# Forgetting attention without the row's constant in its bias, and low key halves over zeros

## The chip, the cores and the metric

The kernel runs on one core of one Trainium2 chip. The metric is the device time in microseconds (us) of one execution; the median of several runs counts. The profile shows one execution: TensorE (PE, with its weight loads as PEld), VectorE (DVE), ScalarE (ACT), GpSimd (POOL) and the queues that issue DMAs (SP among them).

## What is computed

A decoder layer on 512 tokens of width 2048: a mixer of three head groups (12 dilated attention heads "a", 8 forgetting attention heads "b", 4 heads of gated linear attention "c"), a cross-attention, and a gated MLP. All of it is in float32. The part that the change touches is forgetting attention, with heads of 64 and query blocks of 128:

```python
c = jnp.cumsum(jax.nn.log_sigmoid(f_logit.astype(jnp.float32)), axis=1)
...
logits = jnp.einsum('bihd,bjhd->bhij', qn, k,
                    preferred_element_type=jnp.float32) * HEAD_DIM ** -0.5
logits = logits + (cn[..., :, None] - cT[..., None, :])
qpos = n * BLOCK_Q + jnp.arange(BLOCK_Q)
logits = jnp.where(kpos[None, :] <= qpos[:, None], logits, -jnp.inf)
p = jax.nn.softmax(logits, axis=-1)
```

The term cn of the query's own row is the same for all keys of a row, so the softmax does not depend on it.

## The kernel before

Matrix products are made of three matmuls on operands that are split into a rounded high part and a low part (mm3, L375 to L377): high by high, low by high, high by low. Weights stream in by SP's queue; ScalarE rounds them to `whi` (L361 in the mixer, L336 in the MLP), VectorE subtracts to get `wlo` (L362, L337). Five pairs of such splits are held at a time.

The mixer projects first; attention runs behind it in the background. Each head of group a or b is a generator, attend() (L518). Two generators take turns (PAR), and the projections of the following heads call tick() every four blocks of 128 rows, which lets each of the two heads take a step. `behind()` ties each background matmul to the projection matmul ahead of it in the program, and a scheduler then sets the order on each engine; an engine takes its instructions strictly in that order. So a background matmul that has to wait holds up the projections behind it.

A head's steps. The first makes the score operands: `qs` holds the query's high half in the head's 64 rows and its low half in the other 64; `kh` holds the key's high half in both (L526, L527); `kl` holds the key's low half in both: VectorE subtracts it into the head's rows (L529), ScalarE copies it to the other rows (L530). Two matmuls of 128 rows give the scores of a block (L544, L545): the first is q high and q low by k high, the second q high and q low by k low. Then scores(t) for the query blocks t = 0 to 3 and turn(t) in the order s0, s1, t0, s2, t1, s3, t2, t3, one step each. scores(t) adds the bias and takes the row's maximum in one VectorE operation (L547), exponentiates on ScalarE (L548), and scales by the row's sum on VectorE (L549, L550). turn(t) transposes its t + 1 blocks on TensorE (L557), and ScalarE and VectorE split the result into `pth` and `ptl` (L565, L566). At the end eight matmuls multiply with the values into psO (L576, L577), which ScalarE and VectorE add into the mix (L579, L580).

The bias. Group a reads a skewed table. Group b (bias_b, L590) loads the head's cumulated gates as one row to all 128 partitions (`cb`) and builds, for each block, a tile `bb` of cb minus the constant `ci` of each query row: one operation for the blocks to the left (L599), one with the triangle `tri` for the block on the diagonal (L600). `bb` shares its four buffers with the probabilities `pt`. The constants `cnat` come from forget() (L686), a background generator of the gate stage: after the cumulated sum it gives up five turns, then transposes the sums on TensorE (L708) and copies them out on VectorE (L711). gates() (L640; four z matmuls L678, each followed by a log-sigmoid, L506 to L513, and a scan, L683) and rel_bias() (L714; matmuls L738, VectorE L739) share the turns with it.

Of the kernel before, what the change touches and what calls it, by code (L numbers as in the profile page):

```python
# [12 lines left out]
F32 = mybir.dt.float32  # L13
F32R = mybir.dt.float32r
I32 = mybir.dt.int32
AF = mybir.ActivationFunctionType
ALU = mybir.AluOpType
AX = mybir.AxisListType

P = 128  # L20
D = 2048
KT = D // P
S = 512
NT = S // P
# [3 lines left out]
DH = 64  # L28
A_HEADS = 12
B_HEADS = 8  # L30
# [37 lines left out]
PTB = 4  # L68
# [24 lines left out]
SB = 2  # L93
# [136 lines left out]
def _view(t, off, dims):  # L230
    return bass.AP(t.tensor, t.offset + off, [list(t.ap[0])] + [list(d) for d in dims])


class _Trunk:
# [283 lines left out]
    def attend(self, qf, kf, e, vv, bias_of, head, mix):  # L518
        nc, ab = self.nc, self.ab
        a = slice(DH * e, DH * e + DH)  # L520
        o = slice(DH - DH * e, 2 * DH - DH * e)
        qs = ab.tile([P, S], F32R, name="qs", tag="qs", bufs=SB)
        kh = ab.tile([P, S], F32R, name="kh", tag="kh", bufs=SB)
        kl = ab.tile([P, S], F32R, name="kl", tag="kl", bufs=SB)
        nc.scalar.activation(qs[a], qf[a], AF.Copy)
        nc.scalar.activation(kh[a], kf[a], AF.Copy)  # L526
        nc.scalar.activation(kh[o], kf[a], AF.Copy)  # L527
        nc.vector.tensor_tensor(qs[o], qf[a], qs[a].bitcast(F32), op=ALU.subtract)
        nc.vector.tensor_tensor(kl[a], kf[a], kh[a].bitcast(F32), op=ALU.subtract)  # L529
        nc.scalar.activation(kl[o], kl[a].bitcast(F32), AF.Copy)  # L530
        yield
        pth = ab.tile([P, 1280], F32R, name="pth", tag="pth", bufs=PB)
        ptl = ab.tile([P, 1280], F32R, name="ptl", tag="ptl", bufs=PB)
        nm = ab.tile([P, NT], F32, name="nm", tag="nm", bufs=3)
        sm = ab.tile([P, NT], F32, name="sm", tag="sm", bufs=3)
        pts = {}
        bias = bias_of(head)

        def scores(t):
            n = P * (t + 1)  # L540
            sc = self.pst("S")
            tt = slice(t * P, n)
            with self.behind():
                nc.tensor.matmul(sc[:, :n], qs[:, tt], kh[:, :n], start=True, stop=False)  # L544
                nc.tensor.matmul(sc[:, :n], qs[:, tt], kl[:, :n], start=False, stop=True)  # L545
            pt = pts[t] = ab.tile([P, n], F32, name="pt", tag="pt", bufs=PTB, padded_shape=[P, S])
            nc.vector.tensor_tensor_reduce(pt, sc[:, :n], bias(t), -1.0, 1e38, ALU.add, ALU.min, nm[:, t:t + 1])  # L547
            nc.scalar.activation(pt, pt, AF.Exp, scale=-1.0, bias=nm[:, t:t + 1], accum_out=sm[:, t:t + 1])  # L548
            nc.vector.reciprocal(sm[:, t:t + 1], sm[:, t:t + 1])  # L549
            nc.vector.tensor_scalar(pt, pt, sm[:, t:t + 1], None, op0=ALU.mult)  # L550

        def turn(t):
            n, pt = P * (t + 1), pts[t]
            tp = self.pst("T")
            with self.behind():
                for b in range(t + 1):
                    nc.tensor.transpose(tp[:, b * P:(b + 1) * P], pt[:, b * P:(b + 1) * P], self.ident)  # L557
            for b, step in ((0, 384), (2, 128)):
                m = min(t + 1 - b, 2)
                if m > 0:  # L560
                    at = COL[b] + (t - b) * P
                    hv = _view(pth, at, [[step, m], [1, P]])
                    lv = _view(ptl, at, [[step, m], [1, P]])
                    tv = tp[:, b * P:(b + m) * P].rearrange("p (b c) -> p b c", c=P)
                    nc.scalar.activation(hv, tv, AF.Copy)  # L565
                    nc.vector.tensor_tensor(lv, tv, hv.bitcast(F32), op=ALU.subtract)  # L566

        for f, t in ((scores, 0), (scores, 1), (turn, 0), (scores, 2), (turn, 1), (scores, 3), (turn, 2), (turn, 3)):
            f(t)
            yield  # L570
        po = self.pst("O")
        for b in range(NT):
            n = S - b * P
            st = vv[:, b, P * e:P * (e + 1)]
            with self.behind():
                nc.tensor.matmul(po[:, b * P:], st, pth[:, COL[b]:COL[b] + n], start=(b == 0), stop=False)  # L576
                nc.tensor.matmul(po[:, b * P:], st, ptl[:, COL[b]:COL[b] + n], start=False, stop=(b == NT - 1))  # L577
        tmp = ab.tile([P, S], F32, name="ot", tag="pt", bufs=PTB)
        nc.scalar.activation(tmp[a], po[o], AF.Copy)  # L579
        nc.vector.tensor_tensor(mix[a], po[a], tmp[a], op=ALU.add)  # L580
        yield
# [8 lines left out]
    def bias_b(self, h):  # L590
        nc = self.nc
        cb = self.ab.tile([P, S], F32, name="ba", tag="ba", bufs=2)
        nc.scalar.dma_start(out=cb, in_=bass.AP(self.cdr.tensor, self.cdr.offset + h * S, [[0, P], [1, S]]))

        def get(t):
            b = self.ab.tile([P, P * (t + 1)], F32, name="bb", tag="pt", bufs=PTB, padded_shape=[P, S])
            ci = self.cnat[:, t, h:h + 1]
            if t:
                nc.vector.tensor_scalar(b[:, :P * t], cb[:, :P * t], ci, None, op0=ALU.subtract)  # L599
            nc.vector.scalar_tensor_tensor(b[:, P * t:], cb[:, P * t:P * (t + 1)], ci, self.tri,  # L600
                                           op0=ALU.subtract, op1=ALU.add)
            return b

        return get

# [80 lines left out]
    def forget(self):  # L686
        nc, gl = self.nc, self.pre
        fb = self.con.tile([B_HEADS, 1], F32, name="fb")
        with self.tc.issue_after(self.begun.ins):
            nc.gpsimd.dma_start(out=fb, in_=self.d["f_bias"])  # L690
        tp = self.pst("T")
        for t in range(NT):
            nc.tensor.transpose(tp[:B_HEADS, t * P:(t + 1) * P], self.fg[:, t, :B_HEADS], self.ident)
        z = gl.tile([B_HEADS, S], F32, name="fz", tag="zs", bufs=1)
        nc.vector.tensor_scalar(z, tp[:B_HEADS, :], fb, None, op0=ALU.add)
        n = self.neg_log_sigmoid(z, [B_HEADS, S])
        one = gl.tile([B_HEADS, S], F32, name="fone", tag="zs", bufs=1)
        nc.gpsimd.memset(one, 1.0)
        cn = gl.tile([B_HEADS, S], F32, name="cn")
        nc.vector.tensor_tensor_scan(cn, one, n, 0.0, ALU.mult, ALU.add)  # L700
        self.cdr = self.dr.tile([B_HEADS, S], F32, name="cdr")
        nc.scalar.dma_start(out=self.cdr, in_=cn)
        for _ in range(5):
            yield
        tq = self.pst("T")
        with self.behind():
            for t in range(NT):
                nc.tensor.transpose(tq[:, t * B_HEADS:(t + 1) * B_HEADS], cn[:, t * P:(t + 1) * P],  # L708
                                    self.ident[:B_HEADS, :B_HEADS])
        self.cnat = self.con.tile([P, NT, B_HEADS], F32, name="cnat")  # L710
        nc.vector.tensor_copy(self.cnat, tq[:, :NT * B_HEADS].rearrange("p (t h) -> p t h", h=B_HEADS))  # L711
        yield

    def rel_bias(self):  # L714
# [178 lines left out]
    def mixer(self):  # L893
        nc, d, tc = self.nc, self.d, self.tc
# [90 lines left out]
        es_gl.close()  # L985
        self.mab = self.pool(self.es, "mab", "left")
        self.ab = self.pool(es_ab, "ab", "right")
        self.up_pre = {}
        for f in range(2, EARLY):
            self.up_sums(f)  # L990
# [870 lines left out]
```

## Time and profile before

| | us |
|---|---|
| median of 3 runs (2253.62 to 2257.49) | 2253.88 |
| the profiled execution, whole | 2255.07 |
| its span, first to last instruction | 2253.3 |
| TensorE busy in the span | 2233.6 |
| VectorE busy | 1824.1 |
| ScalarE busy | 1243.1 |
| GpSimd busy | 220.8 |

The gate stage lies at about 50 to 95 us of the span, gated linear attention up to about 320, the heads of group a from about 340 to 555, those of group b from there to 700, then the output projection, cross-attention, and the MLP from about 1000 us to the end. A matmul's busy time overlaps with the next one's, so a TensorE that is 99% busy says where it stood idle, not that every matmul ran at its best pace. The granted TensorE clock is full in all slices of the page.

### The profile page before, as it was taken

To read this page: it belongs to the slowest core of one execution; us is meant where nothing else is said; L and a number is where in the kernel's file an instruction comes from. 1 tells how busy PE (TensorE), PEld (TensorE's weight loads), DVE (VectorE), ACT (ScalarE), POOL (GpSimd) and SP (SyncE) were. 2 spreads that over 40 slices of the span, in tenths; PEclk is the share of its full clock that TensorE was granted. 3 is DMA by queue.
4 is the path that set the end of the run, shared out by engine and by line. 5 is a ranking of instruction groups with operands and counts; after the bars stand their busy time and mean duration, and the time that the engine had idled before them with its cause. 6 is when DMAs were issued, how large, how long until landed. Compare 5 with 4: busy or idle time off the path is not lost.

```text
span 2253.3 us, 42653 instructions
## 1 busy us (share of the span) xinstructions
PE 2233.6 (99%) x15902; PEld 2090.3 (93%) x15902; DVE 1824.1 (81%) x3610; ACT 1243.1 (55%) x2552; POOL 220.8 (10%) x308
## 2 busy tenths in 40 slices
PE   9999999999999999999999999999999999999997
PEld 9898898888778888889999999999999999999997
DVE  7826756666797356699999999999999998999887
ACT  7324445655575245585555555555555575747563
POOL 2000101000002011121111111111000020101003
PEclk9999999999999999999999999999999999999999
DMA  6432157322223349589777777877534493836532
GB/s 223 158 98 83 50 149 192 97 89 99 81 88 129 133 151 251 124 207 273 197 212 209 209 211 214 225 221 218 180 132 143 143 337 106 306 127 234 186 129 82
DMA packets 141843, 377.10 MB, mean 167 GB/s; under 512 B 14484, under 2 KB 53732, under 8 KB 140932
## 3 DMA queue, kind: packets, MB, share of 16 engines
q1 hardware_dynamic: 90144, 274.18, 35.0%
q0 software_dynamic: 45728, 89.86, 18.2%
q10 hardware_dynamic: 5764, 10.35, 1.4%
q8 instruction: 124, 2.03, 0.4%
q14 instruction: 83, 0.68, 0.1%
HBM read 347.28 MB, written 91.80 MB: 195 GB/s over the span
## 4 chain that ended last, share of the span: by engine, by line
PE 95%; DVE 2%; ACT 1%; issue 1%; DMA 1%; POOL 0%; DVEq 0%; POOLq 0%; ACTq 0%
PE acc L375 19%; PE acc L377 19%; PE acc L376 19%; PE psC L375 5%; PE psC L376 5%; PE psC L377 5%; PE acc L416 3%; PE acc L418 3%; PE acc L417 3%; PE psD L376 3%; PE psD L375 3%; PE psD L377 3%; PE psT L557 1%; PE psQ L375 1%; PE psS L807 1%; PE psQ L377 1%
## 5 line engine op out<-in xcount | busy, mean ns | idle before, releaser
L336 ACT ACTIVATE whi<-wraw 128x512 fp32r<-128x512 f32 (+2 forms) x814 | 466.3, 603 | 406.6 <-PE acc L376 149.4
L337 DVE TENSOR_TENSOR wlo<-wraw,whi 128x512 fp32r<-128x512 f32 (+2 forms) x814 | 517.0, 656 | 66.8 <-ACT whi L336 62.1
L375 PE MATMUL acc<-sum,whi 128*128 128x256 f32 x1956 | 541.8, 277 | 0.4 <-ACT s L1461 0.3
L377 PE MATMUL acc<-sum,wlo 128*128 128x256 f32 x1956 | 541.6, 277 | 0.3 <-DVE wlo L337 0.2
L376 PE MATMUL acc<-sum,whi 128*128 128x256 f32 x1956 | 541.3, 277 | 0.0
L362 DVE TENSOR_TENSOR wlo<-wraw,whi 128x512 fp32r<-128x512 f32 (+2 forms) x336 | 221.0, 664 | 188.6 <-ACT whi L361 187.6
L377 PEld LDWEIGHTS acc<-sum,wlo 128*128 128x128 f32 x1956 | 367.3, 188 | 1.2 <-DVE wlo L337 1.1
L375 PEld LDWEIGHTS acc<-sum,whi 128*128 128x128 f32 x1956 | 367.1, 188 | 1.2 <-ACT s L1461 0.7
L376 PEld LDWEIGHTS acc<-sum,whi 128*128 128x128 f32 x1956 | 367.3, 188 | 0.0
L361 ACT ACTIVATE whi<-wraw 128x512 fp32r<-128x512 f32 (+2 forms) x336 | 203.0, 609 | 290.7 <-PE acc L376 176.1
L375 PE MATMUL acc<-xhi,whi 128*128 128x512 f32 (+1 forms) x848 | 335.1, 395 | 0.5 <-ACT fg L938 0.5
L377 PE MATMUL acc<-xhi,wlo 128*128 128x512 f32 (+1 forms) x848 | 328.3, 387 | 0.0
L376 PE MATMUL acc<-xlo,whi 128*128 128x512 f32 (+1 forms) x848 | 328.3, 387 | 0.0
L375 PE MATMUL psC<-sum,whi 128*128 128x256 f32 x928 | 256.8, 277 | 0.0
L376 PE MATMUL psC<-sum,whi 128*128 128x256 f32 x928 | 256.7, 277 | 0.0
L377 PE MATMUL psC<-sum,wlo 128*128 128x256 f32 x928 | 256.4, 276 | 0.0
L377 PEld LDWEIGHTS acc<-xhi,wlo 128*128 128x128 f32 x848 | 159.3, 188 | 32.3
L375 PEld LDWEIGHTS acc<-xhi,whi 128*128 128x128 f32 x848 | 159.4, 188 | 29.5 <-ACT fg L938 0.9
L376 PEld LDWEIGHTS acc<-xlo,whi 128*128 128x128 f32 x848 | 159.7, 188 | 28.4 <-DVE xlo L324 0.2
L376 PEld LDWEIGHTS psC<-sum,whi 128*128 128x128 f32 x928 | 174.2, 188 | 0.0
L377 PEld LDWEIGHTS psC<-sum,wlo 128*128 128x128 f32 x928 | 174.2, 188 | 0.0
L375 PEld LDWEIGHTS psC<-sum,whi 128*128 128x128 f32 x928 | 174.2, 188 | 0.0
(406 smaller groups left out, 4340.9 us busy)
## 6 DMA issues: line engine op xcount, KB each, us to landing
wraw<-in_w_up SPq DMA_DIRECT2D x125, 512.0 KB, 6.5
b<-in_w_up SPq DMA_DIRECT2D x42, 512.0 KB, 4.9
wraw<-in_w_o SPq DMA_DIRECT2D x32, 512.0 KB, 3.5
wraw<-in_w_d SPq DMA_DIRECT2D x32, 448.0 KB, 4.4
wraw<-in_w_d SPq DMA_DIRECT2D x36, 384.0 KB, 5.4
wraw<-in_w_qka SPq DMA_DIRECT2D x24, 512.0 KB, 3.6
up<-in_w_up POOLq DMA_DIRECT2D x24, 512.0 KB, 7.3
one<-in_w_d POOLq DMA_DIRECT2D x24, 448.0 KB, 7.3
```

Of the source, the lines that this page charges most:

```text
L336: nc.scalar.activation(hi, r, AF.Copy)
L337: nc.vector.tensor_tensor(lo, r, hi.bitcast(F32), op=ALU.subtract)
L361: nc.scalar.activation(hi, r, AF.Copy)
L362: nc.vector.tensor_tensor(lo, r, hi.bitcast(F32), op=ALU.subtract)
L375: nc.tensor.matmul(out, lh, rh, start=start, stop=False, skip_group_check=more)
L376: nc.tensor.matmul(out, lh, rl, start=False, stop=False, skip_group_check=more)
L377: last = nc.tensor.matmul(out, ll, rh, start=False, stop=stop, skip_group_check=more)
L416: self.nc.tensor.matmul(o, xh[:, tt], wh, start=(k == 0), stop=False)
L417: self.nc.tensor.matmul(o, xh[:, tt], wl, start=False, stop=False)
L418: self.last = self.nc.tensor.matmul(o, xl[:, tt], wh, start=False, stop=(k == KT - 1))
L557: nc.tensor.transpose(tp[:, b * P:(b + 1) * P], pt[:, b * P:(b + 1) * P], self.ident)
L807: nc.tensor.matmul(sc[:rows, c * 64:(c + 1) * 64], kk[:, c * P:c * P + rows], qe[:, c * 64:(c + 1) * 64], start=True, stop=True)
```

## The change

Three things. The bias of group b is cb alone, without the row's constant: get(t) adds the triangle in place to the diagonal block of cb and returns a view of cb. Since that spoils the block for later rows, the query blocks of group b run from last to first (group a keeps its order). So `bb`, `cnat`, its transposes and the five turns in forget() go. And for all heads `kl` holds the low key half over 64 rows of zeros: two tiles (one for the even and one for the odd head of a pair), whose zeros VectorE writes once ahead of group a, take the place of a pool of two, and ScalarE's copy goes. Query low by key low is no longer summed in.

```diff
-        kl = ab.tile([P, S], F32R, name="kl", tag="kl", bufs=SB)
+        kl = self.kl[e]
...
         nc.vector.tensor_tensor(kl[a], kf[a], kh[a].bitcast(F32), op=ALU.subtract)
-        nc.scalar.activation(kl[o], kl[a].bitcast(F32), AF.Copy)
...
         for f, t in ((scores, 0), (scores, 1), (turn, 0), (scores, 2), (turn, 1), (scores, 3), (turn, 2), (turn, 3)):
-            f(t)
+            f(t if bias_of == self.bias_a else NT - 1 - t)
...
-            b = self.ab.tile([P, P * (t + 1)], F32, name="bb", tag="pt", bufs=PTB, padded_shape=[P, S])
-            ci = self.cnat[:, t, h:h + 1]
-            if t:
-                nc.vector.tensor_scalar(b[:, :P * t], cb[:, :P * t], ci, None, op0=ALU.subtract)
-            nc.vector.scalar_tensor_tensor(b[:, P * t:], cb[:, P * t:P * (t + 1)], ci, self.tri,
-                                           op0=ALU.subtract, op1=ALU.add)
-            return b
+            b = cb[:, P * t:P * (t + 1)]
+            nc.vector.tensor_tensor(b, b, self.tri, op=ALU.add)
+            return cb[:, :P * (t + 1)]
...
-        for _ in range(5):
-            yield
-        tq = self.pst("T")
-        with self.behind():
-            for t in range(NT):
-                nc.tensor.transpose(tq[:, t * B_HEADS:(t + 1) * B_HEADS], cn[:, t * P:(t + 1) * P],
-                                    self.ident[:B_HEADS, :B_HEADS])
-        self.cnat = self.con.tile([P, NT, B_HEADS], F32, name="cnat")
-        nc.vector.tensor_copy(self.cnat, tq[:, :NT * B_HEADS].rearrange("p (t h) -> p t h", h=B_HEADS))
...
+        self.kl = [self.ab.tile([P, S], F32R, name="kl%d" % e) for e in range(2)]
+        for kl, o in zip(self.kl, (slice(DH, P), slice(0, DH))):
+            nc.vector.memset(kl[o].bitcast(F32), 0.0)
```

The line numbers of the changed kernel are lower by 1 from L530 on, by 5 behind bias_b (L680 is L675) and by 14 behind forget() (L952 is L938). Three places show how the orders move.

The gate stage on VectorE, around the second head's scan (`gb`, L683 or L678; `ls` and `zs` are steps of the gates' log-sigmoid, `gq` is the q projection of the linear attention, evacuated from TensorE's accumulator). Before:

```order
L513 TENSOR_TENSOR ls_796<-ls_796,ls_797 96x512
L506 TENSOR_SCALAR ls_833<-zs 96x512
L683 SCALAR_TENSOR_TENSOR gb_115<-smask,ls_796 96x512
L507 SCALAR_TENSOR_TENSOR ls_834<-ls_833,zs 96x512
L362 TENSOR_TENSOR wlo<-wraw,whi 128x512
L680 TENSOR_SCALAR zs<-psO,gb 96x512
L509 TENSOR_SCALAR ls_835<-ls_834 96x512
```

In the changed kernel:

```order
L506 TENSOR_SCALAR ls_816<-zs 96x512
L507 SCALAR_TENSOR_TENSOR ls_817<-ls_816,zs 96x512
L675 TENSOR_SCALAR zs<-psO,gb 96x512
L938 SCALAR_TENSOR_TENSOR gq_116<-acc,R 96x512
L938 SCALAR_TENSOR_TENSOR gq_119<-acc,R 32x512
L513 TENSOR_TENSOR ls_778<-ls_778,ls_779 96x512
L678 SCALAR_TENSOR_TENSOR gb_115<-smask,ls_778 96x512
L362 TENSOR_TENSOR wlo<-wraw,whi 128x512
```

The evacuation of the third q projection (`gq_116`), which before stood 14 rows behind that scan, now stands ahead of the second head's L513, its scan and a split of weights; on TensorE the projection matmul that reads this `wlo` is the 15th behind the last one of the third q projection. The z matmuls also moved: the first one stands 8 projection matmuls behind the spreading of the row norm instead of 12.

The change from the first to the second pair of group b on ScalarE: the last turns of the first pair (`pth`), the operands of the second (`kh`, `kl`), the first pair's output (`ot`). Before:

```order
L526 ACTIVATE kh<-kf 64x512
L579 ACTIVATE ot<-psO 64x512
L565 ACTIVATE pth<-psT 128x2x128
L527 ACTIVATE kh<-kf 64x512
L530 ACTIVATE kl<-kl 64x512
L526 ACTIVATE kh<-kf 64x512
L565 ACTIVATE pth<-psT 128x128
L527 ACTIVATE kh<-kf 64x512
L361 ACTIVATE whi<-wraw 128x512
L565 ACTIVATE pth<-psT 128x2x128
L530 ACTIVATE kl<-kl 64x512
L565 ACTIVATE pth<-psT 128x256
```

In the changed kernel:

```order
L526 ACTIVATE kh<-kf 64x512
L527 ACTIVATE kh<-kf 64x512
L578 ACTIVATE ot<-psO 64x512
L564 ACTIVATE pth<-psT 128x2x128
L526 ACTIVATE kh<-kf 64x512
L527 ACTIVATE kh<-kf 64x512
L361 ACTIVATE whi<-wraw 128x512
L564 ACTIVATE pth<-psT 128x128
```

Both kl copies are gone, and the last turn, now that of block 0, needs one copy of 128x128 behind the split of weights, where that of block 3 needed two.

The same place on TensorE: the last turn (`psT`), and the first output matmul (`psO`) that reads its result. Before:

```order
L557 MATMUL psT<-ident,pt 128x128 x4
L375 MATMUL acc<-xhi,whi 128x512
L376 MATMUL acc<-xlo,whi 128x512
L377 MATMUL acc<-xhi,wlo 128x512
L576 MATMUL psO<-pth,vv 128x512
```

In the changed kernel:

```order
L556 MATMUL psT<-ident,pt 128x128
L375 MATMUL acc<-xhi,whi 128x512
L376 MATMUL acc<-xlo,whi 128x512
L377 MATMUL acc<-xhi,wlo 128x512
L575 MATMUL psO<-pth,vv 128x512
```

One transpose stands there instead of four; the three projection matmuls between it and the output are the same.

## The prediction

> **What bounds the kernel now.** I read the page first: the span, the busy time of the engines, and the chain of work that ended last.
>
> ```profile
> span 2253.3 us, 42653 instructions
> PE 2233.6 (99%) x15902; PEld 2090.3 (93%) x15902; DVE 1824.1 (81%) x3610; ACT 1243.1 (55%) x2552; POOL 220.8 (10%) x308
> ...
> PE 95%; DVE 2%; ACT 1%; issue 1%; DMA 1%; POOL 0%; DVEq 0%; POOLq 0%; ACTq 0%
> ```
>
> TensorE (PE) holds 95% of the chain and is idle for 19.7 us of 2253.3. The change takes work from VectorE (DVE) and ScalarE (ACT), and from TensorE four tiny transposes. So it can gain only where TensorE stands waiting for those two. Next the windows, to see how much of the idle time lies in the stages that the change touches (the columns are the stretch in us, its length, then each engine's busy time with its instructions):
>
> ```profile
> 50.00:90.00 40.00, 40.00 (x181) 32.31 (x180) 36.78 (x61) 14.86 (x25) 1.51 (x3) 1.00 0.27 94
> 320.00:340.00 20.00, 20.00 (x92) 16.73 (x91) 9.95 (x21) 8.62 (x19) 3.50 (x5) 1.00 0.77 221
> 340.00:505.00 165.00, 164.61 (x808) 137.84 (x806) 106.83 (x290) 96.67 (x226) 7.16 (x9) 1.00 0.45 125
> 505.00:555.00 50.00, 50.00 (x246) 41.78 (x245) 33.05 (x92) 29.80 (x75) 0.00 (x0) 1.00 0.28 95
> 555.00:700.00 145.00, 142.09 (x694) 115.45 (x693) 117.78 (x329) 94.59 (x219) 2.87 (x4) 1.00 0.25 86
> 730.00:740.00 10.00, 10.00 (x46) 8.29 (x45) 6.36 (x12) 3.56 (x7) 0.00 (x0) 1.00 0.57 210
> ```
>
> 50 to 90 us is the gate stage, 340 to 555 the dilated heads (group a), 555 to 700 the forgetting heads (group b), 730 to 740 a stretch of plain projections. TensorE is idle 0.39 us in the 215 us of group a and 2.91 us in the 145 us of group b. Both run the same attend(); only group b builds a bias, and there VectorE is busy 81% instead of 65%. Who is waited for in group b:
>
> ```profile
> PEld psO L576 <- ACT pth L565: 3.7, 6, 1.9
> ...
> PE psO L576 <- ACT pth L565: 1.8, 2, 1.5
> ...
> PE psT L557 <- DVE pt L550: 0.9, 3, 0.4
> ...
> PEld psS L545 <- ACT kl L530: 0.4, 1, 0.4
> ```
>
> The columns are the total, the times and the longest. Most is the output matmul psO, waiting for the ScalarE copy of the turned probabilities; one such wait is 1.5 us.
>
> Busy time hides short delays, because matmuls overlap, so 2.91 us is the lower end of what group b can give back. For the upper end I take weight loads: they fill 8.29 of 10 us in the plain stretch, where TensorE never waits, and 137.84 of 165, or 83.5%, in group a. At group a's rate 145 us would hold 121.1 us of loads; 115.45 are there, 5.7 less. The Trainium skill (Perfetto Trace Analysis, Identifying the Most-Contended Engine) says that matmul busy share is a poor measure of headroom and weight-load share a good one. Read alone, that rule would see 145 - 115.45 = 29.5 us of room here; this trace speaks against the literal reading, since an unstalled stretch shows 83% and no more. So the room in group b is 2.9 to 5.7 us, 0.13% to 0.25% of the kernel.
>
> **The change, part by part.** First the prices in group b:
>
> ```profile
> L600 DVE SCALAR_TENSOR_TENSOR bb<-ba,cnat,tri 128x128 f32<-128x128 f32 x32 | 11.0, 343 | 0.0
> ...
> L530 ACT ACTIVATE kl<-kl 64x512 fp32r<-64x512 f32 x8 | 5.0, 627 | 1.1 <-DVE kl L529 1.0
> ...
> L566 DVE TENSOR_TENSOR ptl<-psT,pth 128x128 fp32r<-128x128 f32 x17 | 4.8, 283 | 0.7 <-ACT pth L565 0.7
> ...
> L599 DVE TENSOR_SCALAR bb<-ba,cnat 128x384 f32<-128x384 f32 x8 | 3.3, 408 | 0.0
> ...
> L599 DVE TENSOR_SCALAR bb<-ba,cnat 128x256 f32<-128x256 f32 x8 | 2.8, 347 | 0.0
> ...
> L599 DVE TENSOR_SCALAR bb<-ba,cnat 128x128 f32<-128x128 f32 x8 | 2.3, 282 | 0.0
> ```
>
> *Bias, group b.* VectorE loses 11.0 + 3.3 + 2.8 + 2.3 = 19.4 us and gains 32 adds of the triangle, 128x128. No such add is in the trace; it lies between the 282 ns of L599 and the 343 ns of L600, and I take 283 ns, the two-operand row of that size: 9.1 us. Net 10.3 us of 117.78 go. ScalarE loses 8 copies of kl, 5.0 us of 94.59. Both lie beside matmuls; only the waits count.
>
> *Which waits go.* The 1.5 us wait for pth ends a ScalarE queue in which six half-tile copies of the next pair, two splits and the last turns stand in a row. In the new order it has lost the kl copy, 0.63 us, and the last turn is that of block 0: one 128x128 transpose and a single copy of it, where block 3 had four and two copies in a row. The cover of three matmuls ahead of psO has stayed, and so has the weight split ahead of the copy, so I let the 1.8 us fall to 0.7. Of the 0.9 us for pt I take off 0.4, as VectorE is lighter by a tenth, and 0.5 for kl at the start of the stage, where scores no longer wait for a copy of kl. Sum for group b: **-2.0 us** (bounds: 0 to -5.7).
>
> *Group a.* Twelve kl copies go as well. They are waited for once, in the first pair:
>
> ```profile
> PE psS L545 <- ACT kl L530: 0.4, 1, 0.4
> ```
>
> There the second head's kh copy is next in line, so **-0.4 us** is the most, and I take it. The two memsets of 64x512 stand on VectorE between 320 and 340 us, where it is busy 9.95 of 20 us and waits for nothing new; no memset of VectorE is in the trace. Bounded by nothing and by the 64x512 kl copy, 0.63 us, they cost nothing on the path; without that cover it would be 1.3 us at most.
>
> *Gate stage.* The transposes of the cumulated gates go, and with them five turns of a background generator: the z matmuls of the gates and the bias table's matmuls (L678, L738) are now issued earlier. On TensorE:
>
> ```profile
> 53.21 0.40 PE L678 MATMUL psO<-g,w 112*96 112x512 f32 x1
> 53.44 0.40 PE L375 MATMUL acc<-xhi,whi 128*128 128x512 f32 x1
> ...
> 58.90 0.39 PE L678 MATMUL psO<-g,w 112*96 112x512 f32 x1
> 59.22 0.41 PE L708 MATMUL psT<-ident,cn 8*128 8x8 f32 x4
> 59.56 0.50 PE L375 MATMUL acc<-xhi,whi 128*128 128x512 f32 x1
> 59.90 0.40 PE L376 MATMUL acc<-xlo,whi 128*128 128x512 f32 x1
> ```
>
> From a z matmul to the next projection matmul it is 0.23 us without the transposes and 0.66 with them, and one more step is 0.34 instead of 0.23: **-0.5 us**. Against that, two waits that are new. VectorE rows for both:
>
> ```profile
> 51.25 1.39 DVE L672 TENSOR_TENSOR g<-psT,g 16x512 fp32r<-16x512 f32 x2
> ...
> 77.77 0.68 DVE L362 TENSOR_TENSOR wlo<-wraw,whi 128x512 fp32r<-128x512 f32 x1
> ...
> 79.15 0.69 DVE L513 TENSOR_TENSOR ls<-ls,ls 96x512 f32<-96x512 f32 x1
> ...
> 80.10 1.22 DVE L683 TENSOR_TENSOR_SCAN gb<-smask,ls 96x512 f32<-96x512 f32 x1
> ...
> 83.21 1.38 DVE L952 SCALAR_TENSOR_TENSOR gq<-acc,R 96x512 f32<-96x512 f32 x2
> ```
>
> The first z matmul stands four matmuls earlier, at 53.21 - 4 x 0.23 = 52.3, but it needs g, whose second half ends at 51.25 + 1.39 = 52.64: **+0.4 us**, with the projections queued behind it. Then the splits. In the new VectorE order the pair of evacuations of the third q projection stands ahead of an L513, a scan and the wlo that the next projection reads. The pair can start only when its projection has ended, and the matmul that reads that wlo stands 15 behind that end: 15 x 0.23 = 3.45 us. VectorE needs 0.39 (the last matmul's end) + 1.38 + 0.69 + 1.22 + 0.68 = 4.36. So TensorE waits **+0.9 us**, near 83 us (bounds 0 and 1.5, as the wait itself has no row; I take what the rows add up to, and it is more if VectorE comes there late).
>
> *Sum:* -2.0 - 0.4 - 0.5 + 0.4 + 0.9 = -1.6 us. The profiled execution took 2255.07 us, 1.8 more than its span; the sum gives 2253.5 for it. It stood 1.2 us above the median of the runs, 2253.88, so the median should become **2252.3 us**, -0.07%. What a measurement of this kernel can tell from no change is about 0.2%, 4.5 us: the answer is "the same".
>
> **The rivals.**
> *The waits only move* (2254.7): psO's wait is set by the split that stands ahead of the pth copy and not by kl; group b gives back 0, group a nothing, and the gate stage keeps its two new waits, 0.4 + 0.9 - 0.5 = +0.8 with the transposes: 2253.9 + 0.8. For it: the weight split stays ahead of that copy. Against it: 15 us less on the two engines.
>
> *Group b becomes like group a* (2247.7, faster): all 5.7 us come back, and the 0.4 and 0.5, with the wlo wait at nought: -5.7 - 0.4 - 0.5 + 0.4 = -6.2. For it: group a shows 0.39 us idle with the same attend(). Against it: the drain of the last pair, where nothing is left to fill TensorE, is in both. The skill's rule (Perfetto Trace Analysis, the section named) leans this way.
>
> *Block 3 first is too early* (2260.3, slower). In the first pair the turn of block 3 stands only 15 projection matmuls and block 2's scores behind block 3's scores, about 15 x 0.23 + 0.5 = 3.9 us. Its chain:
>
> ```profile
> L362 DVE TENSOR_TENSOR wlo<-wraw,whi 128x512 fp32r<-128x512 f32 x39 | 27.0, 696 | 5.1 <-ACT whi L361 4.4 <-PE psS L545 0.5
> ...
> L548 ACT ACTIVATE pt<-pt,nm 128x512 f32<-128x512 f32 x9 | 6.5, 725 | 1.6 <-DVE nm L547 1.4
> ...
> L548 ACT ACTIVATION_READ_ACCUMULATOR pt<-pt,nm 128x1 f32 x33 | 6.2, 188 | 0.0
> ...
> L547 DVE CUSTOM_DVE_ANT_0 pt<-psS,bb 128x512 f32<-128x512 f32 x8 | 5.5, 684 | 1.2 <-PE psS L545 1.2
> ...
> L549 DVE RECIPROCAL sm<-sm 128x1 f32<-128x1 f32 x33 | 5.2, 158 | 1.5 <-ACT pt L548 1.4
> ...
> L550 DVE TENSOR_SCALAR pt<-pt,sm 128x512 f32<-128x512 f32 x9 | 4.3, 482 | 0.2
> ```
>
> 0.39 for the matmul's end, 0.28 for the add, 0.68, 0.73 + 0.19, 0.16 and 0.48: 2.9 us, a slack of 1.0. It turns into a wait when more than 1.0 us of other VectorE work stands in that queue: one split, 0.70, and the add and reduction of block 2, about 0.28 + 0.55, make 1.5 and a wait of 0.5. If the other heads' turns, which have about 24 matmuls of cover, were late too, at 0.7 us for each of 8 heads it would be 5.6 us, with group b's gain lost and the gate stage's 0.8: 2253.9 + 5.6 + 0.8 = 2260.3. Against it: the second heads have 5.5 us of cover, and group b's VectorE is lighter.
>
> *It does not do what it says*: the orders of all engines show the copies, bias operations and transposes gone, so I give this nothing.
>
> **How the numbers follow.** The forecast has 0.62, the waits that move 0.23, all room back 0.09, block 3 too early 0.06. The first two lie within 0.2% (2249.4 to 2258.4): same 0.85, faster 0.09, slower 0.06. The range takes in group b's bounds short of the last microsecond and, upward, the moved waits with 2 us of block 3's: 2249.0 to 2256.5.
>
> **What would show it.** Right: no L708; in 50 to 90 us TensorE waits about 0.4 us for g and 0.9 us for a wlo; in group b VectorE falls to about 107 us, ScalarE to 90, and the wait psO for pth to under 1 us; every stage after 700 us takes as long as now. Wrong: a wait of psT for pt that has grown over 2 us (block 3 too early), a wait of psS for the bias row, or TensorE idle under 0.5 us in group b (then all room came back).

## The result, and the profile after

| | before | changed |
|---|---|---|
| median (lowest to highest) | 2255.32 us (2253.62 to 2257.49, 6 runs) | 2291.47 us (2289.94 to 3178.67, 6 runs) |
| ratio, with its 95% interval | | 1.0159 [1.0145, 1.0173] |
| span of the profiled execution | 2253.3 us | 2289.7 us |

The change makes the kernel 1.6% slower, where the prediction had 2252.3 us (2249.0 to 2256.5) and the same. (The 3178.67 us are one run at a granted clock of 0.65, which the ratio leaves out; the other five lie between 2289.94 and 2292.73.)

First, the head of the page and the chain of work that ended last, of the changed kernel:

```profile
span 2289.7 us, 42608 instructions
PE 2270.5 (99%) x15898; PEld 2117.9 (92%) x15898; DVE 1823.6 (80%) x3587; ACT 1236.5 (54%) x2532; POOL 223.8 (10%) x308
...
PE 97%; DVE 2%; ACT 1%; DMA 0%; issue 0%; SPq 0%; POOL 0%; DVEq 0%; ACTq 0%
```

TensorE is idle for 19.2 us; before it was 19.7. So the 36 us are not a wait. TensorE is busy for 36.9 us longer, with four matmuls fewer. Next the waits of TensorE in the changed kernel (total us, times, longest), which answer to the rows of the prediction:

```profile
PE acc L377 <- DVE wlo L362: 0.8, 1, 0.8
...
PE psS L543 <- ACT kh L527: 0.4, 1, 0.4
PE psT L556 <- DVE pt L549: 0.4, 2, 0.3
...
PE psO L673 <- DVE g L667: 0.3, 1, 0.3
...
PE psO L575 <- ACT pth L564: 0.2, 1, 0.2
```

The two new waits came at about their size: wlo 0.8 (0.9 was forecast), g 0.3 (0.4). The two that were to shrink did: psT for pt from 0.9 to 0.4 (0.5), psO for pth from 1.8 to 0.2, further than the forecast 0.7. The wait for kh, in group a, was not forecast. And then the windows, of the changed kernel (the columns are as in the prediction):

```profile
555.00:700.00 145.00, 143.82 (x703) 116.34 (x702) 111.25 (x310) 90.49 (x211) 0.00 (x0) 1.00 0.26 87
700.00:1000.00 300.00, 299.68 (x1475) 248.56 (x1474) 178.92 (x318) 150.77 (x291) 44.10 (x47) 1.00 0.57 161
...
1400.00:1795.00 395.00, 395.00 (x3385) 395.00 (x3384) 371.04 (x584) 215.09 (x384) 28.04 (x36) 1.00 0.60 175
```

and of the kernel before:

```profile
700.00:1000.00 300.00, 299.69 (x1525) 253.14 (x1524) 184.55 (x331) 157.32 (x303) 44.09 (x48) 1.00 0.59 166
...
1400.00:1795.00 395.00, 395.00 (x3473) 395.00 (x3472) 377.26 (x598) 220.43 (x394) 27.38 (x36) 1.00 0.60 178
```

Here is the loss. In group b (555 to 700 us) TensorE's idle time fell from 2.91 to 1.18 us. But from 700 us on, where the change touches no instruction, TensorE is as busy as before at the same granted clock (1.00) and gets through fewer matmuls: 1475 instead of 1525, and 3385 instead of 3473 in 395 us of the MLP. That is 395 / 3473 = 113.7 ns for a matmul before and 116.7 ns now. The busy share (99% in both), the weight loads (395 of 395 us in both MLP windows) and the clock row (9 in every slice of both pages) show none of it; only the counts do.

The starts of three kinds of matmul in the two traces date the loss. The first one of the cross-attention's output projection (acc<-coh) starts at 945.8 us before and at 957.1 now, 11.3 late. The first product of two MLP sums (psD<-sum,sum) starts at 2203.2 and at 2239.5, 36.3 late; the last of these 288 matmuls at 2238.0 and 2274.3, still 36.3 late. So the mixer and the cross-attention lose 11.3 us, the MLP 25.0, and 35 us of matmuls whose two operands are both sums lose nothing.

### The profile page after: what moved, and what is told of

It is laid out like the page before. It is cut to its first block, busy times and chain, and to the rows that moved or that the text cites. A ratio compares the mean times of both kernels' runs of the same rounds, so it can differ in the third digit from the quotient of the medians.

```text
span 2289.7 us, 42608 instructions
## 1 busy us (share of the span) xinstructions
PE 2270.5 (99%) x15898; PEld 2117.9 (92%) x15898; DVE 1823.6 (80%) x3587; ACT 1236.5 (54%) x2532; POOL 223.8 (10%) x308
## 4 chain that ended last, share of the span: by engine, by line
PE 97%; DVE 2%; ACT 1%; DMA 0%; issue 0%; SPq 0%; POOL 0%; DVEq 0%; ACTq 0%
PE acc L375 19%; PE acc L377 19%; PE acc L376 19%; PE psC L376 5%; PE psC L375 5%; PE psC L377 5%; PE acc L416 3%; PE acc L418 3%; PE acc L417 3%; PE psD L375 3%; PE psD L376 3%; PE psD L377 3%; PE psT L556 1%; PE psQ L377 1%; PE psQ L376 1%; PE psQ L375 1%
## 5 line engine op out<-in xcount | busy, mean ns | idle before, releaser
L377 PEld LDWEIGHTS acc<-xhi,wlo 128*128 128x128 f32 x848 | 159.6, 188 | 36.3 <-DVE wlo L362 1.2
```

The costliest lines, as they stand in the source:

```text
L377: last = nc.tensor.matmul(out, ll, rh, start=False, stop=stop, skip_group_check=more)
```

## What could have moved

The front of this document lists instructions, and the prediction priced instructions. The diff also moves data. The constants `cnat` were a tile of 4 x 8 floats, 128 bytes in each partition, in the kernel's pool of constants. This pool fills the on-chip memory from one end ("left"), with the pools of weights behind it; the activations' splits fill it from the other end ("right"). Without `cnat` every later left-hand tile stands 128 bytes lower, and the right-hand ones stay. In the allocation of the two compiled programs:

```
                                                 before   changed   (byte address in a partition)
whi (left), the stationary operand                34752     34624
the same, modulo 256                                192        64
xhi, xlo (right), moving operands, modulo 256       192       192
44 of 56 MLP sums (right), moving, modulo 256       128       128
```

I call **distance** the address of the next matmul's stationary operand less the address of the current matmul's moving operand, modulo 256 bytes. Counted over the program, before the change some 2300 matmuls of the mixer (`xhi` or `xlo` moving, 512 columns, weights next) stand at distance 0 and some 9700 of the MLP (a sum moving, 256 columns, weights next) at 64; after it the former stand at 128, and some 8700 of the latter at 192. The other thousand, whose sums lie at the left end and move along, stay at 64. Nearly all products of two sums stand at 0 in both kernels. So do those of the cross-attention's output projection (acc<-coh), whose operands both lie at the left end and moved together: from its first matmul's start to its last's it takes 45.9 us in both kernels (945.8 to 991.7, and 957.1 to 1003.0), so it lost nothing either. The code has strips whose only effect is on addresses, such as an unused tile of 8 floats named `edge` at the right-hand end (L244) and shifts by `PHASE` and `HALF`, parts of a `LINE` of 64 floats (L52 to L56). The front leaves them out, and I didn't weigh them.

So the theories were: **theory 1**, the distance sets the pace of the matmuls; **theory 2**, the new order or the new instructions do; **theory 3**, the absolute address of the weights does.

## Experiments: does the address do it?

*pad128*: the changed kernel, with 128 unused bytes where the constants stood.

```diff
         nc.scalar.dma_start(out=self.cdr, in_=cn)
+        self.con.tile([P, 32], F32, name="pad")
```

> The changed kernel with 128 unused bytes per partition where cnat stood, so that every tile of the left-hand pools has the address it had before the change. Theory 1 (addresses: the matmuls slow down because the weight splits moved by 128 bytes against the activations): 2252 us as forecast, 2250 to 2255, and 512-column matmuls 0.227 us apart. Theory 2 (instructions: the order, the zeros or the in-place adds slow TensorE): stays at 2291 us, matmuls 0.232 us apart. Theory 3 (the absolute address of the left-hand tiles alone): as theory 1.

*before_pad128*: the kernel before, with the same line behind its `cnat`.

```diff
         self.cnat = self.con.tile([P, NT, B_HEADS], F32, name="cnat")
+        self.con.tile([P, 32], F32, name="pad")
```

> The kernel before with 128 unused bytes per partition behind cnat; nothing else differs. It moves the left-hand tiles up by 128 bytes, which puts the weight splits at 64 within a line of 256 bytes, where the change puts them. Theories 1 and 3: about 2291 us, slower by some 36 us. Theory 2: 2255 us, as before.

*edge128*: the changed kernel, with the right-hand strip 128 bytes wider, so that the activations move down instead of the weights moving up.

```diff
-        edge.tile([P, 8], F32, name="edge")
+        edge.tile([P, 40], F32, name="edge")
```

> The changed kernel with the unused tile at the right-hand edge 128 bytes wider, so that the activations move by 128 bytes too: weight splits and activations again stand at the same place within a line of 256 bytes, both at 64. Theory 1 (the distance between the two counts): about 2252 us. Theory 3 (the absolute place of the weight splits counts): about 2291 us. Theory 2: 2291 us.

*pad64*: as pad128 with 64 bytes (`[P, 16]`).

> The changed kernel with 64 unused bytes where cnat stood: weight splits at 128, activations at 192 within a line of 256 bytes, a distance of 64 where before has 0 and the change has 128. Theory 1: not 2291 us again but a time of its own; if the loss grows with the distance, about 2272 us. Theory 2: 2291 us.

| | median us | ratio to before, with its interval | distance, mixer / MLP |
|---|---|---|---|
| pad128 | 2254.93 (11 runs) | 0.9995 [0.9986, 1.0004] | 0 / 64 |
| before_pad128 | 2291.39 (4 runs) | 1.0158 [1.0142, 1.0173] | 128 / 192 |
| edge128 | 2254.69 (10 runs) | 0.9994 [0.9985, 1.0003] | 0 / 64 |
| pad64 | 2310.44 (4 runs) | 1.0240 [1.0226, 1.0254] | 192 / 0 |

(The kernel before took 2256.05 us, 21 runs, beside them.) pad128 is the changed kernel, instruction for instruction and in the same order, and an unused strip takes back the whole loss: theory 2 falls. before_pad128 has no part of the change and loses the same 1.6%. edge128 leaves the weights at the changed kernel's addresses, and the loss is gone: theory 3 falls, the relation between the two ends counts. The windows of pad128:

```profile
555.00:700.00 145.00, 143.71 (x703) 116.88 (x702) 112.92 (x308) 90.71 (x213) 4.06 (x4) 1.00 0.27 89
700.00:1000.00 300.00, 299.68 (x1526) 253.11 (x1524) 184.11 (x330) 157.06 (x302) 43.40 (x47) 1.00 0.60 166
...
1400.00:1795.00 395.00, 395.00 (x3473) 395.00 (x3473) 376.71 (x597) 220.34 (x395) 25.79 (x33) 1.00 0.61 178
```

The counts of the kernel before are back, 3473 among them, and what the change gains is kept: 1.29 us idle in group b instead of 2.91.

pad64 was a miss: I had thought that half the shift would cost about half. (What its expectation calls a distance of 64 is 192 by the definition above, since the weights stand 64 bytes short of the activations.) It costs more than the whole. So the pace doesn't fall steadily with the shift; each distance has a pace of its own. Its window in the MLP:

```profile
1400.00:1795.00 395.00, 395.00 (x3325) 395.00 (x3324) 366.15 (x572) 211.69 (x377) 26.09 (x34) 1.00 0.60 174
```

395 / 3325 = 118.8 ns, at distance 0.

## Experiments: the distance by itself

*micro* leaves the layer out: one stationary tile, of which each matmul takes a slice, and one moving tile, no other engine at work beside TensorE. STEPS are the letters a to p, N is 24.

```diff
+        for n in (512, 256):
+            for i, s in enumerate(STEPS):
+                acc = ps.tile([P, S], F32, name=("big" if n == 512 else "half") + s, tag="acc", bufs=4)
+                for k in range(N):
+                    o = 4 * i + 64 * (k % 5)
+                    nc.tensor.matmul(acc[:, :n], w[:, o:o + P], x[:, :n], start=(k == 0), stop=(k == N - 1))
```

> This kernel leaves the layer out: it holds only matmuls of one stationary and one moving tile. Sixteen groups, a to p, of 24 matmuls of 512 columns, then sixteen of 256 columns; from letter to letter the stationary slice starts 16 bytes later against the moving operand, modulo 256 bytes (a is 0, e 64, i 128, m 192), and no other engine works beside them. Theory 1 (the pace depends on where the next weights lie against the moving operand): the pitch, from one start to the next, goes by the letter: for 512 columns a 227, i 232, m 226 ns, for 256 columns a 120, e 113, m 118 ns, as in the layer at those distances. Rival (the shifted tiles collide with what ScalarE and VectorE read and write beside TensorE): all letters have one pitch, near 226 ns and 113 ns. A difference between letters of under 1 ns speaks for the rival, one of 4 ns and more for theory 1.

In micro's timeline of TensorE each row is a group of 24 matmuls: its start in us, how long it ran, and what it was.

```profile
15.03 5.61 PE L33 MATMUL bigb<-x,w 128*128 128x512 f32 x24
20.48 5.75 PE L33 MATMUL bigc<-x,w 128*128 128x512 f32 x24
26.07 5.76 PE L33 MATMUL bigd<-x,w 128*128 128x512 f32 x24
...
98.50 3.03 PE L33 MATMUL halfa<-x,w 128*128 128x256 f32 x24
101.37 3.01 PE L33 MATMUL halfb<-x,w 128*128 128x256 f32 x24
...
109.87 2.89 PE L33 MATMUL halfe<-x,w 128*128 128x256 f32 x24
112.60 3.02 PE L33 MATMUL halff<-x,w 128*128 128x256 f32 x24
```

From one start to the next, over 24: 227 ns for b, 233 for c, 120 for half a, 114 for half e. The pace goes by the letter with nothing beside it, so the rival (collisions with the other engines) falls. (The first group, biga, isn't used: its first matmuls start 427 ns apart, and only from about 12 us on some 230. The letter m, forecast at 226 ns for 512 columns, came out at 228.9.) These are mean gaps between neighbouring starts at each distance, in the micro kernels and, from all neighbouring pairs of that width in their traces, in the layer's own variants (512 columns: 700 to 800 us, some 430 pairs each; 256 columns: 1500 to 1600 us, some 850):

| distance | 512 columns, micro | in the layer | 256 columns, micro | in the layer |
|---|---|---|---|---|
| 0 | 226.7 (micro2) | 227.1 (before) | 119.7 | 118.9 (pad64) |
| 32 | 233.1 | | 118.4 | 117.9 (pad96) |
| 64 | 233.2 | 233.8 (pad192) | 113.4 | 113.8 (before) |
| 128 | 233.5 | 232.8 (changed) | 120.1 | 118.6 (pad192) |
| 192 | 228.9 | 229.3 (pad64) | 117.7 | 116.7 (changed) |
| 224 | 233.4 | 233.7 (pad96) | 116.8 | |

The layer follows the bare matmuls within 0.8 ns for 512 columns and 1.5 ns for 256, although its windows mix in other distances (over the whole changed kernel a fifth of the pairs of 256 columns). The best distance is another one for each width, 0 (or 16, micro's b) for 512 columns and 64 for 256, and the kernel before had 0 and 64.

To test the table rather than fit it, two more strips were forecast from it, 32 and 64 bytes off the old place.

*pad96* and *pad192*: as pad128 with `[P, 24]` and `[P, 48]`.

> The changed kernel with 96 unused bytes where the constants stood: the weights stand 32 bytes ahead of their old place, most mixer pairs at distance 224, MLP pairs at 32. Theory 1, with the pitches of micro: MLP 118.4 ns (c) where 113.4 (e) was, 5.0 ns on some 8700 pairs, 30 to 42 us by the share that the changed kernel (0.7) and pad64 (0.96) made of such a product; mixer as in the changed kernel, 233 ns (o), some 9 us more. Together 2295 to 2307 us. Rival (32 bytes are too little to matter, only steps of 64 bytes count): 2255, or below the changed kernel's 2291.

> The changed kernel with 192 unused bytes: the weights stand 64 bytes behind their old place, most mixer pairs at distance 64, MLP pairs at 128. Theory 1, with the pitches of micro: MLP 120.1 ns (i) for 113.4, 6.7 ns on some 8700 pairs, 41 to 56 us by the same two shares, and the mixer at 233 ns (e), some 9 us: 2305 to 2321 us. Rival (the loss goes with the distance from the place before, and 64 bytes one way cost as 64 bytes the other, where the mixer lost nothing): 2310, with the mixer's 512 columns at 226 to 227 ns as in pad64.

| | median us (4 runs each) | ratio to before, with its interval |
|---|---|---|
| pad96 | 2306.69 | 1.0222 [1.0207, 1.0238] |
| pad192 | 2310.89 | 1.0242 [1.0225, 1.0259] |

Both lie within what the table gave, 2295 to 2307 and 2305 to 2321, pad96 at the very top. 32 bytes of nothing cost 51 us. And pad192 is not pad64 mirrored: its time is the same, but its mixer has lost too (233.8 ns instead of 229.3), as theory 1 had it.

*micro2* first runs 48 matmuls, so that the slow start is over, then repeats the letters, and has groups of 256 columns that go by turns into two banks.

> The layer is left out, as in micro. First 48 matmuls that let the clock come up, then the sixteen groups of 512 columns again: if the pace is a property of the distance alone, b, l, m and p come out at 227 to 229 ns again and the other letters at 231 to 234; a (distance 0), which the rising clock spoilt in micro, is to show the layer's 227. Then matmuls of 256 columns that go by turns into two banks, one and two: with both weights at distance 0 (AA) the pitch should be 120 ns, with both at 64 (EE) 113. With one at 0 and two at 64 (AE): if the weights of the next matmul count, which are loaded while this one streams, the pitch from one to two is 113 and from two to one 120; if a matmul's own weights count, 120 from one to two and 113 from two to one; if both count alike, both are near 117.

```profile
21.34 5.60 PE L34 MATMUL biga<-x,w 128*128 128x512 f32 x24
26.78 5.61 PE L34 MATMUL bigb<-x,w 128*128 128x512 f32 x24
```

The letters repeated, and a, at distance 0, came out at (26.78 - 21.34) / 24 = 226.7 ns. Of the rest, both weights at distance 0 gave the expected 120.0, and the others missed: with both weights at distance 64 the pitch was 118 ns, not 113; by turns it was 117.5 from one to two and 119.1 back. The distance isn't all. *micro3* took the differences apart:

```diff
+        for s, banks, same, p in (("plain", 1, 0, (16, 16)), ("banks", 2, 0, (16, 16)), ("twice", 1, 1, (16, 16)), ("turns", 1, 0, (0, 16)),
+                                  ("plain0", 1, 0, (0, 0)), ("banks0", 2, 0, (0, 0)), ("twice0", 1, 1, (0, 0))):
...
+            for k in range(2 * N):
+                o = p[k % 2] + 64 * ((k // 2 if same else k) % 5)
+                nc.tensor.matmul(accs[k % banks][:, :256], w[:, o:o + P], x[:, :256], start=(k < banks), stop=(k >= 2 * N - banks))
```

> The layer is left out. In micro2 the weights at distance 64 took 118 ns where they took 113 in micro; two things differed: the matmuls went by turns into two banks, and each slice of weights was loaded twice running. Groups of 48 matmuls of 256 columns take these apart: plain (distance 64, one bank, another slice each time) 113 if micro repeats; banks (the same, two banks) 118 if the banks did it, else 113; twice (one bank, each slice twice running) 118 if the repeated slice did it, else 113. The same three at distance 0 (plain0, banks0, twice0) are 120 throughout if distance 0 is bound by something that neither touches. turns (one bank, distance 0 and 64 by turns): if the next matmul's weights count, 113 from a matmul with weights at 0 to one at 64 and 120 back; if a matmul's own weights count, the reverse; near 117 both ways if both count.

Its timeline (groups of 48; the second "plain" is plain0):

```profile
20.51 5.82 PE L35 MATMUL plain<-x,w 128*128 128x256 f32 x48
26.16 5.82 PE L35 MATMUL banks<-x,w 128*128 128x256 f32 x48
31.82 5.82 PE L35 MATMUL twice<-x,w 128*128 128x256 f32 x48
37.47 5.84 PE L35 MATMUL turns<-x,w 128*128 128x256 f32 x48
43.15 5.92 PE L35 MATMUL plain<-x,w 128*128 128x256 f32 x48
48.91 5.92 PE L35 MATMUL banks<-x,w 128*128 128x256 f32 x48
```

Another miss, and a telling one: plain holds the same matmuls at the same addresses as micro's group e, and takes (26.16 - 20.51) / 48 = 117.7 ns where that took 113.4. Neither the banks nor the repeated slice did it. turns gave 117.5 ns towards weights at 64 and 119.1 towards weights at 0, near the 117.7 and 120.0 of plain and plain0: this speaks for the next matmul's weights, weakly. What differs from micro is what ran just before. *micro4* puts these 24 matmuls behind eight others, at each letter and at 512 columns ("wide"), in two sweeps over the banks:

> The layer is left out. micro's group e and micro3's group plain hold the same matmuls at the same addresses, yet one ran at 113 ns and the other at 118; what differs is the matmuls that ran just before and the accumulator's bank. Here the same 24 matmuls (256 columns, distance 64) come 34 times: behind 8 matmuls at each of the sixteen distances and behind 8 of 512 columns, all this twice, with the accumulator in another bank the second time. If the bank decides, groups of one bank agree and both paces appear, whatever ran ahead. If the history decides (a pace, once taken up, goes on), a group's pace follows the letter ahead of it and is the same in both sweeps: 113 behind d, 118 behind the 512 columns. If neither does, all 34 have one pace, and the difference between micro and micro3 stays open.

Some rows of its timeline, from both sweeps (e0 and e1):

```profile
29.01 2.90 PE L39 MATMUL e0afterc<-x,w 128*128 128x256 f32 x24
...
32.70 2.90 PE L39 MATMUL e0afterd<-x,w 128*128 128x256 f32 x24
...
62.16 2.99 PE L39 MATMUL e0afterl<-x,w 128*128 128x256 f32 x24
...
81.60 2.99 PE L47 MATMUL e0afterwide<-x,w 128*128 128x256 f32 x24
...
92.93 2.99 PE L39 MATMUL e1afterc<-x,w 128*128 128x256 f32 x24
...
96.70 2.89 PE L39 MATMUL e1afterd<-x,w 128*128 128x256 f32 x24
```

A group runs 2.88 to 2.91 us (113 to 114 ns a matmul) or 2.99 (118), with nothing between. In both sweeps it is slow behind a, b, l, m and 512 columns and fast behind the other letters; c alone differs. Slow and fast groups are found in every bank. So at distance 64 there are two paces, and, c apart, the matmuls just before decide which is taken up; it then holds to the group's end (the fast groups come to it within at most five starts). This accounts for both misses: micro2's groups at 64 came behind matmuls at distance 0, as behind a, and micro3's plain behind 512 columns, and here both are slow. In the layer, at that distance, the mean of 113.8 says that most matmuls ran at the fast one: nine in ten of the starts from 1500 to 1600 us are at most 115 ns apart.

## Experiments: the parts of the change, at the old addresses

*kl_only* is the kernel before with the low key half over zeros alone (its edit is below; the two tiles and their memsets are those of the change), *bias_only* is pad128 with the kl copy put back, so with the bias and the block order alone.

```diff
-        kl = ab.tile([P, S], F32R, name="kl", tag="kl", bufs=SB)
+        kl = self.kl[e]
...
-        nc.scalar.activation(kl[o], kl[a].bitcast(F32), AF.Copy)
```

> The kernel before with the low key half over zeros alone; the constants stay, and with them every address that TensorE streams from. Theory 1 for the time: the parts of the change cost nothing, only the addresses do, so 2254 to 2256, not 2291. If it were the kl tiles or their memsets that slowed TensorE, this would be near 2291. For group b (TensorE idle 2.9 us there before, 1.3 with the whole change and the old addresses): if the kl copy on ScalarE held up the turned probabilities, as the prediction had it for part of 1.1 us, idle falls to 1.3 to 2.0 and psO's wait for pth from 1.8 to under 1.0; if the order of the blocks and the lighter bias did it, idle stays at 2.5 to 2.9. In group a the 0.4 us wait for kl is gone.

> The changed kernel with the 128 unused bytes and with the kl copy put back: bias without the constants and query blocks from last to first alone. Theory 1: 2254 to 2256. Group b: if block order and bias made the gain, TensorE is idle 1.3 to 2.0 us there and psO's wait for pth is under 1.0; if the kl copy did, 2.5 to 2.9 us, with the wait for kl (0.4) still there. The waits for g (0.3) and for wlo (0.9) in the gate stage are here, since the transposes and turns are gone; kl_only does not have them.

| | median us (11 runs each) | ratio to before, with its interval | TensorE idle, 555 to 700 us | psO waits for pth |
|---|---|---|---|---|
| before | 2255.28 (21 runs) | | 2.91 us | 1.8 us |
| kl_only | 2255.05 | 0.9998 [0.9990, 1.0007] | 1.97 | 0.9 |
| bias_only | 2256.26 | 1.0004 [0.9995, 1.0013] | 2.72 | 1.5 |
| both (pad128) | 2254.93 | 0.9995 [0.9986, 1.0004] | 1.29 | 0.2 |

None of the three is told apart from the kernel before by its time. Their traces are. Of kl_only the waits and the windows of groups a and b:

```profile
PE psO L575 <- ACT pth L564: 0.9, 1, 0.9
...
PE psS L543 <- ACT kh L527: 0.5, 1, 0.5
```

```profile
340.00:505.00 165.00, 164.48 (x808) 138.12 (x807) 106.20 (x290) 90.71 (x215) 8.16 (x11) 1.00 0.45 125
...
555.00:700.00 145.00, 143.03 (x698) 116.08 (x697) 118.10 (x330) 90.32 (x212) 3.34 (x4) 1.00 0.27 88
```

Of bias_only:

```profile
PE psO L576 <- ACT pth L565: 1.5, 1, 1.5
...
PE psS L545 <- ACT kl L530: 0.4, 1, 0.4
```

The kl copy is the larger part: without it alone psO's wait for pth halves and group b gains 0.94 us. Bias and order alone give 0.19. Together they give 1.62, more than the sum: as long as the copy stands in ScalarE's queue, the shorter last turn waits behind it. ScalarE's rows from the turn before to the last turn's copy, in bias_only and then in pad128:

```profile
595.11 0.39 ACT L565 ACTIVATE pth<-psT 128x256 fp32r<-128x256 f32 x1
596.21 0.63 ACT L530 ACTIVATE kl<-kl 64x512 fp32r<-64x512 f32 x1 [0.72 <-DVE kl L529]
...
598.69 0.26 ACT L565 ACTIVATE pth<-psT 128x128 fp32r<-128x128 f32 x1
```

```profile
595.38 0.38 ACT L564 ACTIVATE pth<-psT 128x256 fp32r<-128x256 f32 x1
595.79 0.63 ACT L526 ACTIVATE kh<-kf 64x512 fp32r<-64x512 f32 x1
...
597.64 0.26 ACT L564 ACTIVATE pth<-psT 128x128 fp32r<-128x128 f32 x1
```

Besides, both have two copies to kh and a split of weights there. With the kl copy it is 3.58 us from one pth to the next, without it 2.26. The 1.3 us between them are 0.63 of copy and 0.72 in which ScalarE stood idle until VectorE had made what it copies, and psO's wait of 1.5 against 0.2 differs by as much. And in group a nothing was won: the wait of 0.4 us for kl became one of 0.5 for kh.

## Why the prediction was wrong

**The step that failed** is the one under "What would show it" that "every stage after 700 us takes as long as now", and behind it the whole of "The change, part by part": it prices `cnat` by the instructions that make and read it, and takes the duration of every other matmul from the trace of before. Freeing 128 bytes moved the weights' splits against the activations, the pitch rose from 227.1 to 232.8 ns for 512 columns and from 113.7 to 116.7 ns in the MLP, and this, which has no term in the sum, is +36 us. The strip alone, in the kernel before, gave 2291.39, and the change with the strip put back 2254.93. None of the rivals contains it. "It does not do what it says", to which the prediction gave nothing, was set aside by the orders of instructions, which don't show an address.

**The terms of the sum.** Where the addresses are kept (pad128), the span is 2252.3 us, 1.0 below before, and the forecast was 1.6 below; these are single executions, and the ratio can't be told from 1. The base of 2253.88 was low as well: it is the median of three runs, six gave 2255.32. By terms:

- Group b, -2.0: idle time fell by 1.62 us with the old addresses and by 1.73 in the changed kernel. The mechanism was right (the last turn no longer stands behind a kl copy), and psO's wait fell further than I had it, to 0.2. The upper bound of 5.7, from the rate of weight loads, wasn't approached: 116.88 us of loads are in the window, where the bound needed 121.1.
- Group a, -0.4: wrong. The prediction itself says that "the second head's kh copy is next in line"; it was, with 0.5 us.
- Gate stage, -0.5 + 0.4 + 0.9 = +0.8: the waits came at 0.3 and 0.8 to 0.9. The first scores of linear attention (psS<-qe,ke) start at 182.0 us before, 183.0 in bias_only, 183.3 in edge128 and 184.0 in pad128. From 50 to 100 us TensorE is idle for 1.2 us in each of these three and not at all before, which is the two waits. The rest of pad128's 2.0 lies ahead of 50 us: TensorE is idle there for 2.66 us instead of 1.55, but edge128, with the same instructions, has 1.97, so this differs between executions.
- The prices: the groups of VectorE instructions in pad128 (count, busy us, mean ns) give the two that the trace of before lacked.

```profile
L596 DVE TENSOR_TENSOR ba<-ba,tri 128x128 f32<-128x128 f32 x32 | 9.0, 283 | 4.1 <-DMA ba<-cdr 4.0
...
L977 DVE MEMSET kl<- 64x512 f32 x2 | 1.0, 485 | 0.2 <-issue 0.2
```

The add costs the 283 ns that were taken for it, the memset 485 within its bounds of 0 and 627, and no wait of TensorE for it is listed. VectorE's busy time in group b fell to 111.25 us and not to about 107: by these rows the bias got 10.4 us cheaper, so 3.9 us of other work came into the window, which now holds 703 matmuls instead of 694.

**The rivals.** "The waits only move" (2254.7) holds, of what sets it apart from the forecast, for group a alone. "Group b becomes like group a" fell, since 1.2 us of idle time are left. "Block 3 first is too early" fell: psT's wait for pt shrank to 0.4 us.

With addresses kept, then, the change is worth nothing that can be measured, as forecast. No version was found that beats the kernel before.

## What to carry to other kernels

A change that frees, adds or resizes a tile also moves every tile placed behind it, so compare the addresses of the operands of the costliest instructions before pricing the instructions, above all where the kernel contains unused strips. When an engine is just as busy and the span grows, divide a stretch of uniform work by its count: here 113.7 against 116.7 ns stood out at once, while busy shares, waits and clock were silent. To judge an edit by itself, first put back, with an unused strip, the bytes that it moved.

## What the runs showed of the hardware

TensorE's pace on float32 operands depends on where the weights lie against the moving operand, modulo 256 bytes: 227 to 234 ns for 512 columns and 113 to 120 for 256, without idle time or clock change in the profile, worth 2255 to 2311 us in this kernel. At the same addresses (256 columns, distance 64) there can be two steady paces, 113 and 118 ns, and the matmuls just ahead decide between them for 16 of the 17 kinds that micro4 put there; behind c its two sweeps differ. The likely reading is that the loading of the next weights and the streaming of the current operand get in each other's way; the controls are only that 288 products of two sums and the cross-attention's output projection, whose operands kept their distance, kept their time, and that "turns" leaned towards the next weights. It is argued, not shown. Open too is what in the matmuls ahead picks the pace, and why the layer's MLP keeps mostly to the fast one, at 113.8 ns.

The Trainium skill (TensorE: Matmul & The Clock Gate, Back-to-back issue gap) gives columns / 2.4 + 2.5 ns as the gap of an isolated warm matmul and names no address; for 512 and 256 columns that makes 215.8 and 109.2 ns, an estimate. No run here reaches it: back to back, with a weight load for each matmul, the best distances are 5% above it for 512 columns and 4% for 256, others up to 8% and 10%; here the measurement decides.
